# A decoder layer in fp32 on TensorE: the start bytes of the moving operands

## The chip, the cores and the metric

The kernel runs on one core of a Trainium2 chip. The metric is the device time of one execution in microseconds, from the first to the last instruction and what lies around them; the time before is the median of three runs. The profile is one further execution, taken by the hardware profiler.

Five engines work side by side, each in its own order: TensorE (PE; its weight loads are listed apart as PEld), VectorE (DVE), ScalarE (ACT), GpSimd (POOL), and SyncE (SP), which issues the transfers. They wait for each other by semaphores.

## The reference

One layer over 512 positions of width 2048, all in float32:

```python
h = x + W_out [ DilatedAttn(q,k,v) || S5(u) ]   # [q|k|v|u] = RMSNorm(x) W_in, 1024 columns each
h = h + (silu(n @ w_gate) * (n @ w_up)) @ w_down  # n = RMSNorm(h), D_FF = 5632
y = RMSNorm(h)
```

The attention has 8 heads of 128 and mixes three dilations; S5 is a diagonal state space layer over 64 groups, followed by a gelu and a gate `sigmoid(y @ w_glu)`.

## The kernel before, in words

Everything is kept transposed: features on the 128 partitions, the 512 positions along the free axis. A product is a chain of matmuls on a 128 x 128 weight block (the stationary operand) and 512 or 256 columns of an activation (the moving operand).

To reach float32 accuracy each operand is split in two parts: `hi`, a copy rounded to the matmul's fp32r type, which ScalarE makes (L90), and `lo`, the rest, which VectorE makes (L91 through the helper at L50). A product of two such pairs is three matmuls, hi x hi (L109), weight hi x activation lo (L110) and weight lo x activation hi (L111), in `mm3` at L108. Every matmul has its own weight load. Weights stream from HBM in pieces of 512 KB (`raw`, 4 buffers), are split into `whi` and `wlo` (5 buffers each, 512 columns), and are used once.

The split activations live in slots. `laid` at L167 takes a slot of 1088 words (4352 bytes) a partition and returns 1024 of them, hi in the first half and lo in the second, from word `o` on:

```python
    t = pool_.tile([128, SLOT], F32R, tag=tag, name=name, bufs=bufs)
    return t[:, o:o + 1024].rearrange("p (a b) -> p a b", a=2)
```

The slots of all pools start at multiples of 256 bytes (two small pads, of 480 bytes and 992, see to it). So the start byte of a moving operand within 256 bytes is 4 x `o`, for hi and for lo alike. The pools are `A0` and `A1` (8 slots each), `B` (8 slots in `ring2`), and in `mp` the tags `a` and `C` (4 slots each). One slot holds different operands in the course of the program.

The stages, in the order of the program:

- `u`, `q`, `k`, `v`: products with the 16 tiles `x0` to `x15` (in A0 and A1, `o` = 0), 512 columns each; the state space layer runs beside `u` and `k`.
- Attention: scores, softmax, transposes and `po`; its 8 results are split into `attn` (A0, `o` = 8).
- `glu`: 8 output tiles, each 8 chunks of `ysp` (B, `o` = 4), 512 columns; gated results go to `ssm` (A1, `o` = 40).
- `oa`: the attention half of W_out, 16 output tiles x 8 chunks of `attn`, 512 columns.
- `os`: the other half with `ssm`, in two passes over 256 columns each (`os0`, `os1`), 16 output tiles x 8 chunks. Behind each pass the norm of its columns follows.
- `gu`: gate and up of one feed-forward tile `f` of 44. They are computed by a scheme with seven products of 256 columns instead of eight, named by their weights A to G. A and B read the operand set `c1` (A0), C reads `c4` (tag C, `o` = 52), D and F read `c3` (A1), E and G read `c2` (B); the sets c1 to c3 have `o` = 48. A product is 8 chunks of 128 features, 24 matmuls, in two halves of 12: in the steady state the order on PE is A, C, B, D, E, F, G for the first half and again for the second, 168 matmuls a tile. The first five tiles (`first`) have A and B ahead of the others, since c2 to c4 are made only when the second pass's norm is known.
- `dn`: behind the first `gu` tile of each later group of four, in the code; on PE it stands between groups: 16 output tiles x 4 chunks of `m` (tag a, `o` = 0), 512 columns, 192 matmuls. There are ten, `dn0` to `dn9`.
- `dl`: the last down product with the last four `m` (`o` = 48), in two passes of 256 columns, and the final norm.

A scheduler decides the order in which the instructions of one engine stand.

Of the kernel before, what the change touches and what calls it, by code (L numbers as in the profile page):

```python
# [35 lines left out]
def _emit(tc, a, y):  # L36
# [4 lines left out]
    def opened(name, **kw):  # L41
        cm = tc.tile_pool(name=name, **kw)
        open_pools[name] = cm
        return cm.__enter__()
# [4 lines left out]
    def tt(out, in0, in1, op, eng=None):  # L49
        (eng or dve).tensor_tensor(out=out, in0=in0, in1=in1, op=op)  # L50
# [23 lines left out]
    def acc(name):  # L74
        return psum.tile([128, 512], F32, tag="acc", name=name, bufs=5)
# [13 lines left out]
    def split(hi, lo, raw):  # L89
        act.activation(hi, raw, AF.Copy)  # L90
        tt(lo, raw, hi.bitcast(F32), ALU.subtract)  # L91
# [21 lines left out]
    def ftile(ps, chunks, acts, name):  # L113
        n = len(chunks)
        for c, src in enumerate(chunks):
            ws = wchunk(src, f"{name}_{c}")
            for k in range(8):
                hi, lo = ws[k // 4]
                sl = slice(128 * (k % 4), 128 * (k % 4) + 128)
                mm3(ps, hi[:, sl], lo[:, sl], acts[8 * c + k], c == 0 and k == 0, c == n - 1 and k == 7)  # L120
# [43 lines left out]
    ring = opened("ring", bufs=1)  # L164
    SLOT = 1088

    def laid(pool_, tag, name, bufs, o):  # L167

        t = pool_.tile([128, SLOT], F32R, tag=tag, name=name, bufs=bufs)
        return t[:, o:o + 1024].rearrange("p (a b) -> p a b", a=2)  # L170

    def slot(tag, name, shift=0):
        return laid(ring, tag, name, 8, shift)
# [123 lines left out]
    for n in (1, 2, 4):  # L297
# [4 lines left out]
        t_ = pt[:, :, :n]  # L302
# [233 lines left out]
    ring2 = opened("ring2", bufs=1, side="right")  # L536
# [20 lines left out]
    ysp = []  # L557
    for b in range(8):
        yt = wpool.tile([128, 512], F32, tag="sq", name=f"yt{b}", bufs=4)
        nc.sync.dma_start(yt, sy[b].rearrange("p i c -> p (i c)"))  # L560
        t_ = laid(ring2, "B", f"ysp{b}", 8, 4)
        split(t_[:, 0, :], t_[:, 1, :], yt)
        ysp.append(t_)


    attn = []
    def scores(h):
        Pb = [slot("A1", f"P{h}_{i}").bitcast(F32) for i in range(2)]
        Tb = [slot("A1", f"PT{h}_{i}").bitcast(F32) for i in range(2)]
        for i in range(4):  # L570
            n = 128 * (i + 1)
            P = Pb[i // 2][:, i % 2, :]
            sps = aux([128, 512], f"sc{h}_{i}")
            pe.matmul(sps[:, :n], qs[h][:, 128 * i:128 * i + 128], ks[h][:, 0:n], start=True, stop=True)
            st = cpool.tile([128, 4], F32, tag="st", name=f"st{h}_{i}", bufs=4)
            dve.tensor_tensor_reduce(out=P[:, :n], in0=sps[:, :n], in1=mask[:, 512 - n:512], scale=1.0, scalar=-3e38,
                                     op0=ALU.add, op1=ALU.max, accum_out=st[:, 0:1])
            ts(st[:, 1:2], st[:, 0:1], -SCALE)
            act.activation(P[:, :n], P[:, :n], AF.Exp, bias=st[:, 1:2], scale=SCALE, accum_out=st[:, 2:3])
            dve.reciprocal(st[:, 3:4], st[:, 2:3])  # L580
            ts(P[:, :n], P[:, :n], st[:, 3:4])
        return Pb, Tb

    nxt = scores(0)
    for h in range(NH):
        Pb, Tb = nxt
        if h + 1 < NH:
            nxt = scores(h + 1)
        po = acc(f"po{h}")
        for step in "t0 t1 t2 p0 t3 p1 p2 p3".split():  # L590
            j = int(step[1])
            w = 512 - 128 * j
            PT = Tb[j // 2][:, j % 2, :]
            if step[0] == "t":
                tp = acc(f"tp{h}_{j}")
                for i in range(j, 4):
                    pe.transpose(tp[:, 128 * (i - j):128 * (i - j) + 128], Pb[i // 2][:, i % 2, 128 * j:128 * j + 128], ident)
                act.activation(PT[:, :w], tp[:, :w], AF.Copy)
            else:
                pe.matmul(po[:, 128 * j:512], vs[j][:, 128 * h:128 * h + 128], PT[:, :w], start=j == 0, stop=j == 3)  # L600
        o = slot("A0", f"attn{h}", 8)
        act.activation(o[:, 0, :], po, AF.Copy)
        tt(o[:, 1, :], po, o[:, 0, :].bitcast(F32), ALU.subtract)
        attn.append(o)


    ssm = []
    for f in range(8):
        ps = acc(f"glu{f}")
        ftile(ps, [a["w_glu"][f]], ysp, f"glu{f}")  # L610
        g_ = wpool.tile([128, 512], F32, tag="sq", name=f"gate{f}", bufs=4)
        act.activation(g_, ps, AF.Sigmoid, bias=bg[:, f:f + 1])
        yt = wpool.tile([128, 512], F32, tag="sq", name=f"yr{f}", bufs=4)
        nc.sync.dma_start(yt, sy[f].rearrange("p i c -> p (i c)"))
        z = wpool.tile([128, NC_, T], F32, tag="sq", name=f"gz{f}", bufs=4)
        tt(z.rearrange("p c i -> p i c"), yt.rearrange("p (i c) -> p i c", i=T), g_.rearrange("p (i c) -> p i c", i=T), ALU.mult)
        o = slot("A1", f"ssm{f}", 40)
        split(o[:, 0, :], o[:, 1, :], z.rearrange("p c i -> p (c i)"))
        ssm.append(o)
    closed("v")  # L620
# [6 lines left out]
    h = [hall[:, f, :] for f in range(KT)]  # L627
# [10 lines left out]

    def comb(tag, name, pool_=None, bufs=8):

        return laid(pool_ or ring, tag, name, bufs, 52 if tag == "C" else 48).rearrange("p a (h t) -> p a h t", h=2)

    early = {}

# [21 lines left out]
    def first_half(k):  # L666
        n_ = laid(mp, "a", f"n1_{k}", 4, 0).bitcast(F32).rearrange("p a (h t) -> p a h t", h=2) if k % 2 == 0 else n1[-1][1]
        n1.append((n_[:, k % 2], n_))
        tc.keep_in_program_order(norm(n1[k][0][:, 0], k, E[0]))
        norm(n1[k][0][:, 1], k + 8, E[0])  # L670
        t_ = comb("A0", f"c1_{k}")
        split(t_[:, :, 0, :], t_[:, :, 1, :], n1[k][0])
        c1.append(t_)
# [96 lines left out]
    for k in range(8):  # L770
        es = E[1]
        x_, y_, z_ = (wpool.tile([128, 2, 256], F32, tag="sq", name=f"{n}_{k}", bufs=4) for n in ("x2", "t12", "t34"))
        norm(x_[:, 0], k + 8, es)
        norm(z_[:, 0], k, es)
        tt(x_[:, 1], x_[:, 0], z_[:, 0], ALU.subtract, pool)
        t2 = comb("B", f"c2_{k}", ring2)
        split(t2[:, :, 0, :], t2[:, :, 1, :], x_)
        tt(y_[:, 0], z_[:, 0], n1[k][0][:, 0], ALU.subtract, pool)
        tt(y_[:, 1], x_[:, 0], y_[:, 0], ALU.subtract, pool)
        t3 = comb("A1", f"c3_{k}")  # L780
        split(t3[:, :, 0, :], t3[:, :, 1, :], y_)
        tt(z_[:, 1], n1[k][0][:, 1], y_[:, 1], ALU.subtract, pool)
        if k % 2 == 0:
            t4 = comb("C", f"c4_{k}", mp, 4)
            c4.append(t4)
        split(t4[:, k % 2, 0, :], t4[:, k % 2, 1, :], z_[:, 1])
        c2.append(t2)
        c3.append(t3)
# [14 lines left out]
    for p in range(NPH):  # L803
        ms = []
        for q in range(4):
            f = 4 * p + q
# [114 lines left out]
```

## Time and profile before

| | us |
|---|---|
| median of 3 runs | 2116.21 |
| lowest and highest | 2115.62, 2118.56 |
| the profiled execution | 2112.28 |
| its span, first to last instruction | 2110.5 |
| PE busy | 2053.3 (97%) |
| PEld busy | 1858.4 (88%) |
| DVE busy | 1535.6 (73%) |
| ACT busy | 865.6 (41%) |
| mean granted TensorE clock | 0.986 |

A matmul's recorded duration reaches from its start to the modelled end of its last column, and the next one starts before that: in steady state a 256-column matmul is listed with 276 ns and the next starts 113 ns behind its start. What counts for the time is the distance of the starts. An engine listed as busy throughout may still be slower or faster per instruction, so the tables of stretches are read together with the counts and with the mean duration of one.

### The profile page before, as it was taken

What the parts mean: (1) busy time and instruction counts of PE and PEld (TensorE: products, weight loads), DVE (VectorE), ACT (ScalarE), POOL (GpSimd) and SP (SyncE); (2) the same over time, 40 slices, a digit from 0 to 9 for tenths busy, and PEclk for the clock granted to TensorE, in tenths of its full rate; (3) what the DMA queues carried; (4) which work ended last, traced back from release to release, by engine and by line L of the source; (5) the groups of instructions that cost most, each with busy time, mean ns of one, the idle gap of its engine ahead of it and who ended that gap; (6) DMA issues with size and microseconds to landing.
All of it is one profiled execution on the core that took longest, in us unless ns stands there. A gap on an engine that the chain in (4) does not pass through costs nothing.

```text
span 2110.5 us, 35164 instructions
## 1 busy us (share of the span) xinstructions
PE 2053.3 (97%) x13522; PEld 1858.4 (88%) x13522; DVE 1535.6 (73%) x2932; ACT 865.6 (41%) x1523; POOL 198.1 (9%) x172
## 2 busy tenths in 40 slices
PE   7899999999999979999999999999999999999996
PEld 5688888877889979899998989899998989999896
DVE  8835897555436989687786968687686868778686
ACT  5222222346325645344443535344352535444354
POOL 4533102300002360000000000000000000000002
PEclk9999999999999989999999999999999999999998
DMA  6443234623324614323232223323232332323232
GB/s 222 127 121 112 92 102 140 178 81 125 125 91 169 206 65 140 121 100 120 82 129 90 101 101 120 111 90 130 85 124 83 111 110 101 120 88 124 90 121 80
DMA packets 117193, 244.24 MB, mean 116 GB/s; under 512 B 39040, under 2 KB 57312, under 8 KB 117024
## 3 DMA queue, kind: packets, MB, share of 16 engines
q1 hardware_dynamic: 107808, 239.88, 33.8%
q10 hardware_dynamic: 9216, 2.10, 0.5%
q8 instruction: 106, 1.74, 0.3%
q14 instruction: 63, 0.52, 0.1%
HBM read 229.77 MB, written 9.03 MB: 113 GB/s over the span
## 4 chain that ended last, share of the span: by engine, by line
PE 87%; DVE 7%; issue 2%; DMA 1%; ACT 1%; SPq 0%; POOL 0%; DVEq 0%; ACTq 0%; POOLq 0%
PE gu L109 12%; PE gu L111 12%; PE gu L110 12%; PE dn L110 7%; PE dn L109 7%; PE dn L111 7%; PE lps L437 1%; PE q L111 1%; PE q L110 1%; PE oa L111 1%; PE oa L109 1%; PE oa L110 1%; PE q L109 1%; PE v L550 1%; PE v L552 1%
## 5 line engine op out<-in xcount | busy, mean ns | idle before, releaser
L110 PE MATMUL dn<-m,whi_dn 128*128 128x512 f32 x640 | 249.0, 389 | 0.0
L109 PE MATMUL dn<-m,whi_dn 128*128 128x512 f32 x640 | 248.8, 389 | 0.0
L111 PE MATMUL dn<-m,wlo_dn 128*128 128x512 f32 x640 | 248.8, 389 | 0.0
L50 DVE TENSOR_TENSOR h<-h,dn 128x512 f32<-128x512 f32 x160 | 109.9, 687 | 172.5 <-PE dn L111 171.3
L90 ACT ACTIVATE whi_dn<-raw_dn 128x512 fp32r<-128x512 f32 x160 | 100.9, 632 | 240.5 <-PE dn L110 208.2
L50 DVE TENSOR_TENSOR raw_r<-raw_r,raw_r 128x512 f32<-128x512 f32 x264 | 182.5, 691 | 2.2
L111 PEld LDWEIGHTS dn<-m,wlo_dn 128*128 128x128 f32 x640 | 120.2, 188 | 24.9
L109 PEld LDWEIGHTS dn<-m,whi_dn 128*128 128x128 f32 x640 | 120.2, 188 | 24.6
L110 PEld LDWEIGHTS dn<-m,whi_dn 128*128 128x128 f32 x640 | 120.2, 188 | 24.5
L50 POOL TENSOR_TENSOR h<-h,ssf 128x256 f32<-128x256 f32 x12 | 10.7, 920 | 1300.1 <-ACT ssf L160 1300.1
L50 DVE TENSOR_TENSOR wlo_dn<-raw_dn,whi_dn 128x512 fp32r<-128x512 f32 x160 | 109.8, 687 | 17.6 <-ACT whi_dn L90 16.5
L109 PE MATMUL gu<-c,whi_C 128*128 128x256 f32 x352 | 99.8, 284 | 1.9 <-ACT c L90 1.6
L111 PE MATMUL gu<-c,wlo_E 128*128 128x256 f32 x352 | 98.8, 281 | 2.8 <-DVE wlo_E L50 2.8
L109 PE MATMUL gu<-c,whi_D 128*128 128x256 f32 x352 | 98.3, 279 | 2.7 <-ACT whi_D L90 2.7
L109 PE MATMUL gu<-c,whi_E 128*128 128x256 f32 x352 | 98.5, 280 | 2.4 <-ACT whi_G L90 1.7
L111 PE MATMUL gu<-c,wlo_D 128*128 128x256 f32 x352 | 98.5, 280 | 2.0 <-DVE wlo_D L50 2.0
L111 PE MATMUL gu<-c,wlo_C 128*128 128x256 f32 x352 | 99.5, 283 | 0.5 <-DVE wlo_C L50 0.5
L110 PE MATMUL gu<-c,whi_C 128*128 128x256 f32 x352 | 99.6, 283 | 0.1
L110 PE MATMUL gu<-c,whi_E 128*128 128x256 f32 x352 | 98.3, 279 | 0.0
L110 PE MATMUL gu<-c,whi_D 128*128 128x256 f32 x352 | 98.0, 278 | 0.0
L109 PE MATMUL gu<-c,whi_F 128*128 128x256 f32 x352 | 97.7, 277 | 0.0
L109 PE MATMUL gu<-c,whi_G 128*128 128x256 f32 x352 | 97.5, 277 | 0.2 <-ACT whi_G L90 0.2
(323 smaller groups left out, 6673.1 us busy)
## 6 DMA issues: line engine op xcount, KB each, us to landing
raw_r<-w_gu SPq DMA_DIRECT2D x176, 512.0 KB, 3.6
raw_dn<-w_down SPq DMA_DIRECT2D x80, 512.0 KB, 4.1
raw_os<-w_out SPq DMA_DIRECT2D x32, 512.0 KB, 3.4
raw_q<-w_q SPq DMA_DIRECT2D x16, 512.0 KB, 3.5
raw_k<-w_k SPq DMA_DIRECT2D x16, 512.0 KB, 3.4
raw_v<-w_v SPq DMA_DIRECT2D x16, 512.0 KB, 3.7
raw_oa<-w_out SPq DMA_DIRECT2D x16, 512.0 KB, 3.5
raw_u<-w_u SPq DMA_DIRECT2D x15, 512.0 KB, 4.7
```

The lines of the kernel that those rows point to most:

```text
L50: (eng or dve).tensor_tensor(out=out, in0=in0, in1=in1, op=op)
L90: act.activation(hi, raw, AF.Copy)
L109: pe.matmul(ps, wh, x[:, 0, :], start=first, stop=False)
L110: pe.matmul(ps, wh, x[:, 1, :], start=False, stop=False)
L111: pe.matmul(ps, wl, x[:, 0, :], start=False, stop=last)
L437: pe.matmul(lps[:, g, :], tm_[:, :, :, g].rearrange("p i q -> p (i q)"), U[:, 8 * b + g, :], start=True, stop=True)
L550: pe.matmul(pss[m], xs[kt][:, 0, ms], wh, start=kt == 0, stop=False)
L552: pe.matmul(pss[m], xs[kt][:, 1, ms], wh, start=False, stop=kt == 15)
```

## The change

Four start offsets go; no other line changes. The order of instructions on PE, DVE, ACT, POOL and SP is the same row for row, and the slots are at the same addresses.

```diff
-        t_ = laid(ring2, "B", f"ysp{b}", 8, 4)
+        t_ = laid(ring2, "B", f"ysp{b}", 8, 0)
...
-        o = slot("A0", f"attn{h}", 8)
+        o = slot("A0", f"attn{h}")
...
-        o = slot("A1", f"ssm{f}", 40)
+        o = slot("A1", f"ssm{f}", 48)
...
-        return laid(pool_ or ring, tag, name, bufs, 52 if tag == "C" else 48).rearrange("p a (h t) -> p a h t", h=2)
+        return laid(pool_ or ring, tag, name, bufs, 48).rearrange("p a (h t) -> p a h t", h=2)
```

In bytes: `ysp` goes from 16 to 0, `attn` from 32 to 0, `ssm` from 160 to 192, and `c4`, the operand of product C, from 208 to 192. Behind it every operand read in 256 columns starts at byte 192 of its slot (or 1024 and 2048 bytes further), and every one read in 512 columns at byte 0.

## Rows read from the trace of the kernel before

**Rows 1.** The page: span, busy time of the engines.

```profile
span 2110.5 us, 35164 instructions
PE 2053.3 (97%) x13522; PEld 1858.4 (88%) x13522; DVE 1535.6 (73%) x2932; ACT 865.6 (41%) x1523; POOL 198.1 (9%) x172
```

**Rows 2.** Five stretches: busy time of each engine, granted clock, DMA share.

```profile
core 0: us, PE busy (x) PEld busy (x) DVE busy (x) ACT busy (x) POOL busy (x), PEclk, DMA share, GB/s
640.00:685.00 45.00, 45.00 (x377) 45.00 (x377) 28.67 (x48) 25.90 (x48) 11.33 (x14) 1.00 0.52 177
698.00:734.00 36.00, 34.32 (x278) 33.13 (x278) 35.78 (x63) 22.43 (x45) 14.11 (x13) 1.00 0.54 182
760.00:800.00 40.00, 28.37 (x166) 25.58 (x166) 38.26 (x57) 17.19 (x32) 22.27 (x20) 0.79 0.23 79
800.00:856.00 56.00, 54.23 (x455) 53.16 (x456) 54.18 (x100) 29.73 (x51) 0.00 (x0) 1.00 0.38 134
901.10:978.00 76.90, 76.90 (x673) 76.90 (x672) 64.93 (x114) 39.68 (x66) 0.00 (x0) 1.00 0.33 115
```

**Rows 3.** Matmuls by shape: count, busy us, mean ns; last two: 745 to 757, 2055.5 to 2070.3.

```profile
L109 PE MATMUL dn<-m,whi_dn 128*128 128x512 f32 x640 | 248.8, 389 | 0.0
L110 PE MATMUL glu<-ysp,whi_glu 128*128 128x512 f32 x64 | 25.2, 394 | 0.0
L110 PE MATMUL oa<-attn,whi_oa 128*128 128x512 f32 x128 | 50.6, 395 | 0.0
L110 PE MATMUL os<-ssm,whi_os 128*128 128x256 f32 x256 | 72.2, 282 | 0.0
L109 PE MATMUL gu<-c,whi_C 128*128 128x256 f32 x352 | 99.8, 284 | 1.9 <-ACT c L90 1.6 <-DVE gt L50 0.2
L109 PE MATMUL gu<-c,whi_F 128*128 128x256 f32 x352 | 97.7, 277 | 0.0
...
L110 PE MATMUL gu<-c,whi_A 128*128 128x256 f32 x12 | 3.4, 281 | 0.0
...
L111 PE MATMUL dl<-m,wlo_dl 128*128 128x256 f32 x45 | 12.3, 276 | 0.0
```

**Rows 4.** Timeline of PE behind `dn3`: start us, duration us, instruction; first of five blocks.

```profile
1141.97 0.28 PE L109 MATMUL gu<-c,whi_A 128*128 128x256 f32 x1
...
1143.39 0.28 PE L109 MATMUL gu<-c,whi_C 128*128 128x256 f32 x1
...
1144.81 0.28 PE L109 MATMUL gu<-c,whi_B 128*128 128x256 f32 x1
...
1146.19 0.28 PE L109 MATMUL gu<-c,whi_D 128*128 128x256 f32 x1
...
1151.63 0.28 PE L109 MATMUL gu<-c,whi_A 128*128 128x256 f32 x1
```

**Rows 5.** Timeline of PE in the fourth tile's E and F, and in `dl`.

```profile
839.64 0.28 PE L110 MATMUL gu<-c,whi_E 128*128 128x256 f32 x1
...
841.41 0.28 PE L110 MATMUL gu<-c,whi_G 128*128 128x256 f32 x1
...
2083.80 0.39 PE L109 MATMUL dl<-m,whi_dl 128*128 128x256 f32 x1 [1.17 <-DVE h L50]
2084.03 0.28 PE L110 MATMUL dl<-m,whi_dl 128*128 128x256 f32 x1
...
2085.91 0.28 PE L111 MATMUL dl<-m,wlo_dl 128*128 128x256 f32 x1
```

**Rows 6.** Timeline of PE: ends of the first and of the last group.

```profile
901.10 0.28 PE L109 MATMUL gu<-c,whi_A 128*128 128x256 f32 x1
...
978.00 0.39 PE L109 MATMUL dn<-m,whi_dn 128*128 128x512 f32 x1
...
1985.05 0.28 PE L109 MATMUL gu<-c,whi_A 128*128 128x256 f32 x1
...
2044.44 0.28 PE L109 MATMUL dl<-m,whi_dl 128*128 128x256 f32 x1
```

## The prediction

> **What bounds the kernel now.** I read the page's engine shares first, then a table of stretches, then the matmuls grouped by shape, then the timeline of single matmuls. The shares: TensorE is busy for 97% of the span, weight loads for 88%, VectorE for 73% [rows 1]. The stretches show where that means a bound [rows 2]. From 901.1 to 978 us, the first of ten such groups of four gate/up tiles, PE is busy for 76.90 of 76.90 us and VectorE for 64.93: no wait, every nanosecond on a matmul counts. The first `os` pass (640 to 685) is the same. The second `os` pass (698 to 734) and the making of the operands after the norm (760 to 800) are VectorE's: 35.78 of 36 us and 38.26 of 40, PE idle beside it. From 800 to 856 both are near full (54.23 and 54.18 of 56).
>
> So the question is the distance from one matmul to the next, and whether the start address of the moving operand sets it. The groups by shape [rows 3] have durations: a 512-column matmul takes 389 ns in `dn` (byte 0), 394 in `glu` (byte 16), 395 in `oa` (byte 32). A 256-column one takes 277 ns in `gu` F (byte 192), 284 in `gu` C (byte 208) and 282 in `os` (byte 160). That alone reads as: the four odd offsets cost 5 to 7 ns a matmul, and the change takes this away.
>
> The next rows say that this reading is not enough. At byte 192 there are two paces, not one. In rows 3 the `A` products between 745 and 757 us, at byte 192, take 281 ns; the `dl` products between 2055.5 and 2070.3, at byte 192, take 276; same clock, no wait in either. The timeline of the first tile behind `dn3` [rows 4] shows what chooses. A starts at 1141.97, C at 1143.39, B at 1144.81, D at 1146.19, and the second A at 1151.63. Twelve A's (byte 192) take 1.42 us, 118 ns each; twelve C's (byte 208) 1.42 us, 118; twelve B's (byte 192 again) 1.38 us, 115 on average, the first four near 119 and the rest at 113; and the 48 of D, E, F, G 5.44 us, 113.3 each. So A behind a 512-column product runs at the slow pace although its offset is the "good" one, and the pace falls to the fast one only behind C. All ten groups of tiles that follow a `dn` begin so; the tiles that follow a `gu` tile begin fast.
>
> **Does the slow pace end by itself?** Everything hangs on this. The runs at byte 192 in which it appears with no C in them: 745 to 757 [rows 3], E and F from 839.64 to 841.41 (15 matmuls in 1.77 us), and the closing product, which restarts at 2083.80 after a wait of 1.17 us on VectorE and then holds 1.88 us for 16 matmuls from 2084.03 to 2085.91 [rows 5], and so on to 2091. In all some 300 matmuls at the slow pace, ended by a wait, by C or by the end; none falls to the fast pace alone, and none of the stretches at the fast pace rises alone. Together with A's twelve the three measured pieces are 5.07 us for 43 matmuls, 117.9 ns. It looks like two stable paces of the same stream, kept by whatever the matmul's read and the weight load beside it do to each other, and the pace is inherited. C at byte 208 is slow itself, but whatever pace enters it, the fast one leaves. For 512 columns at byte 0 I see no second pace: `dn` ends at 389 ns whatever came before.
>
> **The change, part by part.** No instruction is added, removed or reordered on any engine; slots and their bases stay. Only start bytes inside the slot move. The writers (ScalarE and VectorE, eight of a kind per stage) get no price: they lie beside a full PE in every stage but the VectorE-bound ones, and there only `c4`'s eight halves move.
>
> 1. `ysp` 16 to 0: 3 x 64 = 192 matmuls, 394 to 389 ns: -1.0 us, on the path.
> 2. `attn` 32 to 0: 3 x 128 = 384 matmuls, 395 to 389: -2.3 us, on the path.
> 3. `ssm` 160 to 192, 768 matmuls. The first pass is entered from a 512-column product at byte 0, as A is entered from `dn`, so I expect the slow pace. Before, 45.00 us hold 377 matmuls, of which two had started earlier [rows 2]: 120.0 ns each, against 117.9: 384 x 2.1 = -0.8 us (bounds 0, and 384 x 6 = -2.3 at the fast pace). The second pass is VectorE's; of its 0.8 us I take -0.2, for the tiles ahead of 698 us.
> 4. `c4` 208 to 192 in the first five tiles. Between 800 and 856 there are 455 matmuls; were all to go from 113.3 to 117.9, that is +2.1 us, with 1.77 us of PE idle to hide it, and C's own gain against it. Bounds -0.5 and +2.1; I take +1.0, nearer to the full price since VectorE is as late as PE there.
> 5. `c4` in the 39 tiles from 901.10 on. This is the large term. Before: a group of four takes 978.00 - 901.10 = 76.90 us; nine such (the others agree to 0.02) are 692.1; the last three tiles run from 1985.05 to 2044.44, 59.39 us, with 15 `dl` matmuls among their 504 [rows 6]. Together 751.5 us for 6567 matmuls, 114.4 each. After: the group still enters through A at the slow pace, since `dn` and A are untouched. C at 192 is then twelve more matmuls of the same kind, and nothing is left in the group that gives back the fast pace. 6567 x 117.9 = 774.2 us: **+22.7 us**. PE has no wait there to hide it in, and VectorE, with 12 us to spare in each group, gets only more slack.
> 6. The closing product: some 40 matmuls up to its first wait, +0.2; behind it every restart may take either pace (bounds -0.7 and +0.7).
>
> Sum: -1.0 - 2.3 - 0.8 - 0.2 + 1.0 + 22.7 + 0.2 = +19.6 us. The profiled execution took 2112.28 us (span 2110.5), so 2131.9 for its like; it lies 3.9 us under the median of the three timed runs, 2116.21, and on that scale the forecast is 2135.8, **2136 us: slower by 0.9%**.
>
> **A rule against it.** Neighbouring products of one tile, equal in columns and clock, stand at 277 and 284 ns with only the start byte between them [rows 3]. The Trainium skill, "TensorE: Matmul & The Clock Gate", section "Step-by-step: what each phase is for", holds that the moving operand and the weight load have independent read ports, so that loading the next weights takes no read bandwidth from the running matmul; the Trainium skill, "SBUF — State Buffer", section "Specifications (TRN2)", gives lines of 16 bytes. By these all the offsets here, multiples of 16, are alike and the change does nothing, 2116 us; the trace disagrees by the 7 ns just named. It is rival N below.
>
> **Rivals.**
> - B, the plain reading: byte 192 is fast and the slow pace does not outlive A. Then every 256-column matmul goes to 113.3: term 5 is 6567 x 113.3 = 744.1, -7.4; terms 1 and 2 as above, -3.3; `os` -2.3 and -0.7; the first tiles -0.5; in all -14.2, 2102 us. For it: most of the trace at byte 192 is fast. Against: those rows all stand behind a C or a wait.
> - P, the slow pace lasts for part of a group. With a share s of the 6567 slow, term 5 is 744.1 + 30.2 s - 751.5; with the other terms (-3.1) the sign turns at s = 0.35. Above it, 2116 to 2131; below, 2105 to 2116. The eight slots of `c4` begin at other bases than `c1`'s, which could still move the pace.
> - N, nothing moves: the paces belong to the products and their place in the program, not to the offset, so all stay as they are: 2116. For it: each odd offset occurs in one product only. Against it: `attn` lies in the slots in which `x` lay, and `dn` at byte 0 is 6 ns shorter than `oa` [rows 3].
> - W, on top of the forecast the half-clock stretch grows: between 760 and 800 the granted clock is 0.79 [rows 2], so part ran at 1.2 GHz while PE waited for VectorE. If it lasts 10 us longer at half pace, +5: 2141.
>
> **How the numbers follow.** Forecast 0.76, B 0.08, P 0.08, N 0.04, W 0.04. The forecast's own range is 2130 to 2140 (terms 3, 4, 6 at their ends, and some 2 us of scatter among the timed runs). Downward I take in N and the upper part of P, upward W: 2114 to 2142, which leaves out B and the low part of P. About 0.2% (4 us) is what a measurement of this kernel can tell from no change. Slower by more: the forecast, W and most of P, 0.83; faster: B and the low end of P, 0.11; same 0.06.
>
> **What would show it.** In the changed kernel's profile: `gu` D, E, F, G at 281 ns instead of 277 and the group of four from A to the next `dn` at 79.2 us instead of 76.90 (term 5); `oa` and `glu` at 389 (terms 1, 2); `os` in the first pass at 281 (term 3). If D to G stand at 276 behind C, term 5 is wrong and with it the sign; if C alone stays at 281 or more, the offset is not what made it slow.

## The result, and the profile after

The changed kernel takes 2136.26 us (median of 4 runs, 2135.12 to 2136.65) beside 2115.91 (4 runs, 2113.49 to 2118.56) of the kernel before on the same chip: a ratio of 1.0095 with the interval 1.0078 to 1.0112, slower by 20 us. The profiled execution of it took 2136.65 us.

The page after, to be held against [rows 1]:

```profile
span 2134.9 us, 35164 instructions
PE 2078.5 (97%) x13522; PEld 1884.5 (88%) x13522; DVE 1540.4 (72%) x2932; ACT 865.4 (41%) x1523; POOL 198.6 (9%) x172
```

The counts are the same. PE and its loads are busier by 25 and 26 us, about as much as the span grew (24), VectorE by 5: the same matmuls take longer.

The stretches after, with the columns of [rows 2]; the borders are moved to the same places of the program, and the first row is the start of the program:

```profile
core 0: us, PE busy (x) PEld busy (x) DVE busy (x) ACT busy (x) POOL busy (x), PEclk, DMA share, GB/s
0.00:150.00 150.00, 129.19 (x649) 103.91 (x650) 104.89 (x194) 52.98 (x95) 69.64 (x57) 0.90 0.53 160
...
647.00:685.00 38.00, 38.00 (x325) 38.00 (x325) 23.87 (x40) 21.68 (x41) 10.79 (x13) 1.00 0.53 182
699.00:735.00 36.00, 33.50 (x278) 32.22 (x278) 35.99 (x64) 23.24 (x48) 15.45 (x13) 1.00 0.54 190
762.00:802.00 40.00, 28.32 (x164) 25.42 (x162) 38.10 (x56) 17.10 (x31) 22.18 (x20) 0.79 0.23 79
802.00:858.00 56.00, 54.41 (x444) 53.16 (x445) 52.71 (x98) 28.50 (x49) 0.00 (x0) 0.97 0.39 132
904.43:983.57 79.14, 79.14 (x673) 79.14 (x672) 65.46 (x114) 39.62 (x66) 0.00 (x0) 1.00 0.33 112
```

The last row answers to 901.10 to 978.00 of [rows 2]: the same 672 matmuls, PE without a gap in both, and 79.14 us in place of 76.90. VectorE is busy for the same 65 us.

The matmuls by shape after (count, busy us, mean ns), as in [rows 3]:

```profile
L109 PE MATMUL dn<-m,whi_dn 128*128 128x512 f32 x640 | 248.8, 389 | 0.0
L110 PE MATMUL glu<-ysp,whi_glu 128*128 128x512 f32 x64 | 24.9, 389 | 0.0
L110 PE MATMUL oa<-attn,whi_oa 128*128 128x512 f32 x128 | 49.8, 389 | 0.0
L110 PE MATMUL os<-ssm,whi_os 128*128 128x256 f32 x256 | 71.7, 280 | 0.0
L109 PE MATMUL gu<-c,whi_C 128*128 128x256 f32 x352 | 99.5, 283 | 1.6 <-ACT c L90 1.6
L109 PE MATMUL gu<-c,whi_F 128*128 128x256 f32 x352 | 100.2, 285 | 0.0
```

`glu` and `oa` went to 389 ns, as `dn`. `C` stayed where it was, 284 to 283, although its offset was corrected; `F`, whose operand was not touched, went from 277 to 285. (The means of `gu` hold a few matmuls that start after a wait; inside a group one takes 281.)

The timeline of PE after: the two ends of the first group, and then the tile that [rows 4] show before the change, the first behind the third `dn` (`dn2` when counted from `dn0`; [rows 4] and the prediction call it `dn3`); first matmul of a block each time:

```profile
904.42 0.28 PE L109 MATMUL gu<-c,whi_A 128*128 128x256 f32 x1
...
983.57 0.39 PE L109 MATMUL dn<-m,whi_dn 128*128 128x512 f32 x1
...
1149.76 0.28 PE L109 MATMUL gu<-c,whi_A 128*128 128x256 f32 x1
...
1151.17 0.28 PE L109 MATMUL gu<-c,whi_C 128*128 128x256 f32 x1
...
1152.59 0.28 PE L109 MATMUL gu<-c,whi_B 128*128 128x256 f32 x1
...
1154.00 0.28 PE L109 MATMUL gu<-c,whi_D 128*128 128x256 f32 x1
...
1155.41 0.28 PE L109 MATMUL gu<-c,whi_E 128*128 128x256 f32 x1
...
1159.65 0.28 PE L109 MATMUL gu<-c,whi_A 128*128 128x256 f32 x1
```

Twelve matmuls of A, of C, of B and of D take 1.41 or 1.42 us each, 118 ns a matmul; half a tile takes 9.89 us where it took 9.66. The 113 ns of D to G are gone from the whole group, and from the three tiles behind it: every group lasts 79.15 us from its first A to the next `dn`.

The difference by stages, each measured from the start of its first matmul to that of the next stage's (us, before to after): `u`, here with the 6 us ahead of its first matmul, 154.17 to 160.15; `q` 117.40 both; `k` to attention 232.51 and 232.52; `glu` 45.44 to 44.54; `oa` 89.60 to 87.04; `os0` 46.08 to 45.23; `os1` 49.40 to 49.12; first five tiles and `dn0` 166.50 to 168.43; nine groups of four, 76.90 to 79.15 each; each `dn` between them 43.53 to 43.52; last three tiles 59.39 to 61.13; the rest of the closing product and the end 66.06 to 65.32. `u`'s 6 us are not the change's: nothing in it is touched, and the same stage took between 154.2 and 162.1 us over the thirteen profiles. Where it is long, the granted clock at its start is lower: the first 150 us have 0.93 where `u` took 154.2 and 0.89 where it took 161.9 and 162.1. It is 0.90 in the stretch above, and in the kernel before:

```profile
0.00:150.00 150.00, 128.06 (x668) 104.52 (x669) 106.09 (x195) 53.45 (x96) 69.76 (x57) 0.93 0.54 161
```

From `k`'s first matmul to the end, which leaves that out, the difference is 1838.94 to 1857.32, **+18.4 us**. This number, called the tail below, is the better measure for kernels with a single run. It still holds the scatter of the stages in which VectorE is late and of the closing product, some us: e3 and e11 below differ by 0.97 us in the stage that was edited, and by 5.2 in their tails.

### The profile page after: what moved, and what is told of

Read it like the earlier page. It is cut to its first block, busy times and chain, and to the rows that moved or that the text cites. A ratio compares the mean times of both kernels' runs of the same rounds, so it can differ in the third digit from the quotient of the medians.

```text
span 2134.9 us, 35164 instructions
## 1 busy us (share of the span) xinstructions
PE 2078.5 (97%) x13522; PEld 1884.5 (88%) x13522; DVE 1540.4 (72%) x2932; ACT 865.4 (41%) x1523; POOL 198.6 (9%) x172
## 4 chain that ended last, share of the span: by engine, by line
PE 88%; DVE 6%; issue 2%; DMA 1%; ACT 1%; POOL 0%; SPq 0%; DVEq 0%; ACTq 0%; POOLq 0%
PE gu L109 13%; PE gu L111 13%; PE gu L110 12%; PE dn L111 7%; PE dn L110 7%; PE dn L109 7%; PE lps L437 1%; PE q L111 1%; PE q L110 1%; PE q L109 1%; PE v L550 1%; PE v L552 1%; PE k L109 1%; PE k L110 1%; PE k L111 1%
## 5 line engine op out<-in xcount | busy, mean ns | idle before, releaser
L50 DVE TENSOR_TENSOR wlo_dn<-raw_dn,whi_dn 128x512 fp32r<-128x512 f32 x160 | 109.8, 687 | 20.3 <-ACT whi_dn L90 19.1
L109 PE MATMUL gu<-c,whi_C 128*128 128x256 f32 x352 | 99.5, 283 | 1.6 <-ACT c L90 1.6
L111 PE MATMUL gu<-c,wlo_F 128*128 128x256 f32 x352 | 100.0, 284 | 0.2 <-DVE wlo_F L50 0.2
L109 PE MATMUL gu<-c,whi_F 128*128 128x256 f32 x352 | 100.2, 285 | 0.0
L110 PE MATMUL gu<-c,whi_F 128*128 128x256 f32 x352 | 100.0, 284 | 0.0
```

The source lines that it names most:

```text
L109: pe.matmul(ps, wh, x[:, 0, :], start=first, stop=False)
L110: pe.matmul(ps, wh, x[:, 1, :], start=False, stop=False)
L111: pe.matmul(ps, wl, x[:, 0, :], start=False, stop=last)
```

## The experiments

All have the same instructions in the same order on each engine as the two kernels; only start bytes differ (in e7 and e10 the size of the weights' tiles too). The slow pace is 117.8 ns from start to start of 256-column matmuls, the fast one 113.3. Each ratio is to runs of the kernel before on the same chip; a kernel without a ratio has one run, and its time holds the scatter of `u`. `dn`, `oa`, `os0` and the group of four are in us, for the first of its kind (of `dn`, the first that nothing interrupts, `dn1`).

| kernel | time, us | ratio to before (interval) | tail, us | group of four | `dn` | `oa` | `os0` |
|---|---|---|---|---|---|---|---|
| before | 2115.91 | | 1838.9 | 76.90 | 43.53 | 89.60 | 46.08 |
| after | 2136.26 | 1.0095 (1.0078 to 1.0112) | 1857.3 | 79.15 | 43.52 | 87.04 | 45.23 |
| e1: `c4` alone | 2137.83 | 1.0107 (1.0090 to 1.0124) | 1860.4 | 79.15 | 43.52 | 89.60 | 46.08 |
| e2: all but `c4` | 2114.98 | 0.9992 (0.9980 to 1.0005) | 1835.8 | 76.90 | 43.53 | 87.04 | 45.23 |
| e3: one slot at 208 | 2107.51 | 0.9963 (0.9952 to 0.9974) | 1834.2 | 76.50 | 43.53 | 87.04 | 45.23 |
| e4: last chunk of `dn` at 208 | 2117.27 | | 1838.8 | 76.16 | 44.56 | 87.04 | 45.23 |
| e5: `m`, `attn` at 192 | 2115.66 | | 1840.5 | 76.16 | 44.80 | 89.60 | 43.53 |
| e6: everything at 0 | 2149.86 | | 1874.9 | 80.63 | 43.55 | 87.04 | 46.07 |
| e7: weights at 16 | 2160.72 | | 1880.2 | 79.74 | 44.80 | 87.04 | 45.62 |
| e8: `m`, `attn` at 64 | 2141.80 | | 1860.7 | 79.15 | 43.96 | 87.91 | 45.22 |
| e9: `m`, `attn` at 128 | 2124.74 | | 1843.4 | 76.16 | 44.80 | 89.59 | 43.52 |
| e10: weights at 16 ahead of the group | 2133.05 | 1.0084 (1.0068 to 1.0099) | 1859.3 | 79.15 | 43.52 | 87.04 | 45.23 |
| e11: e3 and one slot of `ssm` | 2108.95 | 0.9962 (0.9949 to 0.9976) | 1829.0 | 76.50 | 43.53 | 87.04 | 44.26 |

### The change in two halves

e1 is the kernel before with one edit:

```diff
-        return laid(pool_ or ring, tag, name, bufs, 52 if tag == "C" else 48).rearrange("p a (h t) -> p a h t", h=2)
+        return laid(pool_ or ring, tag, name, bufs, 48).rearrange("p a (h t) -> p a h t", h=2)
```

Expected:

> Only c4 moves from byte 208 to 192; ysp, attn and ssm stay at 16, 32 and 160. Theory (the slow pace is inherited from dn and only C at 208 ended it): the loss is c4's alone, +1.0 in the first tiles, +22.7 in the 39 tiles, +0.2 at the end, so 2116 + 24 = 2140 us; a group of four from A to the next dn takes 79.2 us, products D to G 281 ns. Rival (the loss comes from the pace in which glu, oa and os leave the engine, that is from the other three offsets): c4 alone gains its own 1056 x 5 ns, about 2110 us, the group 76.2.

e2 is the changed kernel with that line put back, so that only `ysp`, `attn` and `ssm` have moved. Expected:

> ysp, attn and ssm move, c4 stays at byte 208. Theory: terms 1 to 3 alone, -1.0 -2.3 -0.8 -0.2 = -4.3, so 2112 us; glu and oa at 389 ns, os in its first pass at 281, the group of four unchanged at 76.90 us. Rival (the loss comes from these three): 2136 us, the group at 79.

The ends of the first group in e1's timeline of PE:

```profile
907.01 0.28 PE L109 MATMUL gu<-c,whi_A 128*128 128x256 f32 x1
...
986.15 0.39 PE L109 MATMUL dn<-m,whi_dn 128*128 128x512 f32 x1
```

and in e2's:

```profile
902.73 0.28 PE L109 MATMUL gu<-c,whi_A 128*128 128x256 f32 x1
...
979.63 0.39 PE L109 MATMUL dn<-m,whi_dn 128*128 128x512 f32 x1
```

79.14 and 76.90 us: `c4`'s offset alone makes the loss, and with `c4` at 208 the group is as it was. In the tails the halves add up: +21.4 for e1 and -3.2 for e2, +18.2 together, where the whole change has +18.4. e2's gain was expected at 4.3 us; `glu`, `oa` and `os0` did shorten (0.92, 2.56 and 0.85 us), but the stages behind them, `os1` and the first five tiles, where VectorE is late, are 0.67 and 0.75 longer in its profile. The total is not separable from no change: 0.9992, the interval holds 1.

### How little of byte 208 the fast pace needs

e3 is the changed kernel with one of the four slots of `c4` at byte 208:

```diff
-        return laid(pool_ or ring, tag, name, bufs, 48).rearrange("p a (h t) -> p a h t", h=2)
+        return laid(pool_ or ring, tag, name, bufs, 52 if name == "c4_2" else 48).rearrange("p a (h t) -> p a h t", h=2)
```

Expected:

> As the changed kernel, but one of the four c4 slots (chunks 2 and 3, six matmuls of the first half of C) lies at byte 208, the others at 192. Theory (any matmuls at 208 end the slow pace): only the first 28 matmuls of a group are slow, then every tile pays some 10 x 5 ns; the group takes about 76.45 us, -0.45 x 9.75 = -4.4, and with -4.3 from the other three about 2107 us, faster than both kernels. Rival (a whole C of 24 at 208 is needed, or its slots at both parities): the group stays at 79.2, 2136 us.

e3's timeline of PE; the row at 905.62 is the first of the six matmuls of this tile that read the slot at 208:

```profile
903.50 0.28 PE L109 MATMUL gu<-c,whi_A 128*128 128x256 f32 x1
...
904.91 0.28 PE L109 MATMUL gu<-c,whi_C 128*128 128x256 f32 x1
...
905.62 0.28 PE L109 MATMUL gu<-c,whi_C 128*128 128x256 f32 x1
...
906.33 0.29 PE L109 MATMUL gu<-c,whi_B 128*128 128x256 f32 x1
...
907.04 0.28 PE L109 MATMUL gu<-c,whi_B 128*128 128x256 f32 x1
...
980.00 0.39 PE L109 MATMUL dn<-m,whi_dn 128*128 128x512 f32 x1
```

Twelve of A and six of C at 118 ns (2.12 us), six at 208 in 0.71 us (118), six more behind them in 0.71, and then 113.3. The other three tiles of the group enter fast, and each has its own six matmuls at 208 and the six behind them at about 119: 76.50 us in all. So 24 of the 672 matmuls are at 208, and the first six of them end the slow pace. The kernel is 8.9 us faster than before in the medians (2116.40 in the 19 runs of before on that chip): nine groups shorter by 0.40 would be 3.6 of it, `glu`, `oa` and `os0` 4.3, and the last three tiles 0.3. Its profile has all of these, but is longer by 3.5 in `os1`, the first five tiles and the closing product, so that the tail is only 4.7 shorter; how the 8.9 us divide is not shown.

### What `dn` hands over

e4 is the changed kernel with the last of `dn`'s four chunks at 208, so that each output tile of `dn` ends with three matmuls at 208:

```diff
-        o = laid(mp, "a", f"m{f}", 4, 48 * (f >= 4 * (NPH - 1)))
+        o = laid(mp, "a", f"m{f}", 4, 48 if f >= 4 * (NPH - 1) else 52 if f % 4 == 3 else 0)
```

Expected:

> As the changed kernel, but the last of the four m that a dn product reads lies at byte 208 instead of 0, so that each dn ends with three matmuls of 512 columns at 208. It costs 48 x 5 ns in each of ten dn, +2.4 us. Theory (the pace of a group is inherited from how the last dn matmul ends): the group may now start at the fast pace and then keeps it, 76.15 us, 2116 - 4.3 - 7.4 - 0.5 + 2.4 = 2106 us. Rival (the step from 512 to 256 columns alone sets the slow pace): the group stays at 79.2, 2139 us.

e4's timeline of PE, the end of a `dn` and the group behind it:

```profile
903.42 0.40 PE L109 MATMUL dn<-m,whi_dn 128*128 128x512 f32 x1
...
904.13 0.28 PE L109 MATMUL gu<-c,whi_A 128*128 128x256 f32 x1
...
904.47 0.28 PE L109 MATMUL gu<-c,whi_A 128*128 128x256 f32 x1
...
980.29 0.39 PE L109 MATMUL dn<-m,whi_dn 128*128 128x512 f32 x1
```

The first three A's take 0.34 us, 113 each, and the group 76.16 us, 672 x 113.3: the fast pace throughout, with all of A to G at 192 as in the changed kernel. So A was slow for what stood ahead of it. The price was underrated: `dn` costs 1.03 us more, not 0.24, since the nine matmuls behind the three also go slower (224 to 238 ns apart where `dn` at byte 0 has 226.7). That leaves the total where the kernel before is.

e5, e8 and e9 put all of `m` and of `attn` at one other multiple of 64, 192, 64 and 128:

```diff
-        o = slot("A0", f"attn{h}")
+        o = slot("A0", f"attn{h}", 48)
...
-        o = laid(mp, "a", f"m{f}", 4, 48 * (f >= 4 * (NPH - 1)))
+        o = laid(mp, "a", f"m{f}", 4, 48)
```

with 16 and 32 in place of the 48 in e8 and e9 (the last four `m` kept at 48). Expected:

> As the changed kernel, but m of every dn and attn of oa lie at byte 192 too, so no product from oa on steps from byte 0 to byte 192 any more (glu, u, q, k, v stay at 0). Theory (the pace of a group comes from how dn hands over, not from the step in columns): if 512 columns at 192 run at 227 ns as they do at 0, a group of four starts and stays at the fast pace, 76.15 us instead of 79.15, os in its first pass at 276 instead of 281, in all 2136 - 9.75 x 3.0 - 1.7 = 2105 us. Rival (the step from 512 to 256 columns sets the slow pace wherever both start): 79.15 us, 2136 us. Third case: 512 columns at 192 have a slow pace of their own; then dn lies above 43.5 us.

> As the changed kernel, but attn and the m of every dn lie at byte 64, the operands of 256 columns stay at 192. Theory (the start bytes of dn's and oa's last matmuls set the pace of what follows): the group of four is either 76.16 us (fast, as behind byte 192) or 79.15 (slow, as behind byte 0), with nothing between, and os in its first pass 43.5 or 45.2 in the same way. If 512 columns at 64 run at 227 ns (dn 43.5, oa 87.0) and hand over the fast pace, all stages are at their best: 2136 - 29.2 - 1.7 = 2105 us. Rival (the pace behind dn is set by something else than its start byte, and byte 192 is special by being the same as what follows): 79.15 and 45.2, 2136 us.

> The same with attn and m at byte 128. Theory: again 76.16 or 79.15 and 43.5 or 45.2, and the pace of the 512 columns at 128 tells whether multiples of 64 bytes share the 227 ns of byte 0 (192 did not: 231 to 236). 2105 us if they do and hand over the fast pace. Rival: 79.15 and 45.2 whatever the byte, so long as it is not 192: 2136 us.

`dn` in e5's matmuls by shape:

```profile
L109 PE MATMUL dn<-m,whi_dn 128*128 128x512 f32 x640 | 252.9, 395 | 0.0
```

and in e9's:

```profile
L109 PE MATMUL dn<-m,whi_dn 128*128 128x512 f32 x640 | 252.6, 395 | 0.0
```

512 columns at 128 or 192 take 395 ns instead of 389 (44.80 us for 192, 233 apart), and the group that follows has the fast pace from its first matmul, 76.16. At 64 they cost 43.96, and the group is slow, 79.15. The first and last rows of e9's first group:

```profile
908.66 0.28 PE L109 MATMUL gu<-c,whi_A 128*128 128x256 f32 x1
...
984.82 0.40 PE L109 MATMUL dn<-m,whi_dn 128*128 128x512 f32 x1
```

The rival of e9, that only 192 would hand the fast pace over, is wrong: 128 does so as well. In `oa` and `os0` the same pairs return: `oa` at 0 or 64, `os0` 45.2; `oa` at 128 or 192, `os0` 43.5. Wherever all of A to G are at 192 and the weights at 0 (after, e1, e4, e5, e8 to e10), a group has one of two lengths, 76.16 or 79.15, and what ran ahead of it picks which. Against the changed kernel, e5's `dn` loses ten times 1.28 us and its `oa` 2.56, while its groups gain nine times 2.99 and `os0` 1.70; that brings it back to the kernel before (tail +1.6) and no further.

### Is it the byte, or the stream?

e6 moves all 256-column operands to byte 0 as well:

```diff
-        o = slot("A1", f"ssm{f}", 48)
+        o = slot("A1", f"ssm{f}")
...
-        return laid(pool_ or ring, tag, name, bufs, 48).rearrange("p a (h t) -> p a h t", h=2)
+        return laid(pool_ or ring, tag, name, bufs, 0).rearrange("p a (h t) -> p a h t", h=2)
...
-        o = laid(mp, "a", f"m{f}", 4, 48 * (f >= 4 * (NPH - 1)))
+        o = laid(mp, "a", f"m{f}", 4, 0)
```

Expected:

> As the changed kernel, but the operands read in 256 columns lie at byte 0 as well (ssm, c1 to c4, the last four m), so all moving operands start at byte 0. Theory (two paces belong to the stream of weight load and matmul, not to byte 192): 113.3 and 117.9 ns show again, and whichever the entry gives is kept: 2136 us if dn hands over the slow one, 2105 if the fast one. Rival (256 columns at 0 have one pace only): every product, behind a wait too, has the same mean duration, 276 or more.

The ends of the first group in e6's timeline:

```profile
901.96 0.28 PE L109 MATMUL gu<-c,whi_A 128*128 128x256 f32 x1
...
982.59 0.40 PE L109 MATMUL dn<-m,whi_dn 128*128 128x512 f32 x1
```

80.63 us for 672 matmuls, 120.0 ns each. At byte 0 the 256-column stream has one pace, slower than both of byte 192, and it does not depend on the entry: of the 384 matmuls of `dl`, many of them behind a wait, 349 have the next one 120 ns behind them and none 113. So two paces are not a property of any 256-column stream; the start byte decides whether there are two.

e7 leaves the moving operands of `mm3` as in the changed kernel and starts the split weights 16 bytes into their tiles, all but the early ones of the first tiles and those of `dl`. (In `v` the weights are the moving operand; it runs there at the 232 ns that `glu` had at byte 16 before the change.)

```diff
-        hi, lo = (wpool.tile([128, 512], F32R, tag=t, name=f"{t}_{name}", bufs=HB) for t in ("whi", "wlo"))
+        hi, lo = (wpool.tile([128, 576], F32R, tag=t, name=f"{t}_{name}", bufs=HB)[:, 4:516] for t in ("whi", "wlo"))
```

(and likewise the two that are made by hand for the first product). Expected:

> As the changed kernel, but the split weights of wsplit lie 16 bytes into slots of 2304 bytes (the early and the last weights stay), so that the distance between the start of the weight load and that of the moving operand is what it was for an operand 16 bytes lower, while the operand's own start is unchanged. Theory A (what counts is the distance between the two reads): the matmuls change their duration, 512 columns at 0 from 389 to 394 or so and 256 columns at 192 to 282 or so as c4 at 208 had, without the fast pace of 276. Theory B (the moving operand's own start byte counts): as the changed kernel, 389 and 281, 2136 us.

By shape in e7, `dn` and `oa`:

```profile
L110 PE MATMUL dn<-m,whi_dn 128*128 128x512 f32 x640 | 254.4, 397 | 0.0
...
L110 PE MATMUL oa<-attn,whi_oa 128*128 128x512 f32 x128 | 49.8, 389 | 0.0
```

Neither theory had this: A has the longer `dn`, but not the `glu` and `oa` that stay. The weight's start byte does take part: 512 columns at byte 0, which had one pace before, now have two, 227 ns in `glu` and `oa` (44.59 and 87.04 us) and 233 in `dn` (44.80 us). The larger tiles are not the reason, for e10 below has them too, with `dn` at 43.52. The group is at 79.74, 118.7 a matmul.

Both paces stand within one product of e7, `q`, at a granted clock of 1.00 each time:

```profile
159.53 0.39 PE L109 MATMUL q<-x,whi_q 128*128 128x512 f32 x1
...
164.97 0.39 PE L109 MATMUL q<-x,whi_q 128*128 128x512 f32 x1
...
179.43 0.40 PE L109 MATMUL q<-x,whi_q 128*128 128x512 f32 x1
...
182.23 0.40 PE L109 MATMUL q<-x,whi_q 128*128 128x512 f32 x1
```

The 24 matmuls of the first pair are 226.7 ns apart; the 12 of the second, behind several pauses of PE and a stretch at the granted clock 0.50, 233.3. Operands and weights have the same start bytes in both, so the bytes alone do not set the pace here.

e10 tries to use that: the weights of the last 24 matmuls of each `dn` and of `oa` at 16, all others at 0, to have the group entered by a slower product:

```diff
-        hi, lo = (wpool.tile([128, 512], F32R, tag=t, name=f"{t}_{name}", bufs=HB) for t in ("whi", "wlo"))
+        o = 4 if name.startswith("oa15_") or name.startswith("dn") and "_7_" in name else 0; hi, lo = (wpool.tile([128, 576], F32R, tag=t, name=f"{t}_{name}", bufs=HB)[:, o:o + 512] for t in ("whi", "wlo"))
```

Expected:

> As the changed kernel with all operands at 0 and 192, but the split weights of each dn's last chunk (its last two output tiles, 24 matmuls) and of oa's last output tile lie 16 bytes into their slots; slots of 2304 bytes for all weights. Theory (the pace of the group comes from how the last matmuls before it end, and the weight load's start byte takes part in that): those 24 matmuls run near 233 ns, +0.15 us per dn, and what follows takes one of the two paces: fast, 76.16 us a group and 43.5 in os, 2136 - 29.2 - 1.7 + 1.6 = 2107 us, or slow again, 79.15 and 45.2, 2138. Rival (the operand's start byte alone counts): 79.15 and 45.2, no change in dn, 2136.

e10's first group:

```profile
904.06 0.28 PE L109 MATMUL gu<-c,whi_A 128*128 128x256 f32 x1
...
983.21 0.39 PE L109 MATMUL dn<-m,whi_dn 128*128 128x512 f32 x1
```

No effect: `dn` 43.52, the group 79.15, the ratio within the interval of the changed kernel's. A 512-column stream that runs at 227 stays there when the weights move to 16, so the slower `dn` of e7 does not come from the weights' byte alone: with `q` in e7, this says that 512 columns too can keep a pace that they enter with.

### The version that beats both

e11 adds to e3 the same trick for `os`: the first slot of `ssm` at 208.

```diff
-        o = slot("A1", f"ssm{f}", 48)
+        o = slot("A1", f"ssm{f}", 48 if f else 52)
```

Expected:

> As the run with one c4 slot at byte 208, and the first of the eight ssm also at 208 instead of 192. Theory (a few matmuls at 208 end the slow pace in any 256-column stream): in the first pass of os each output tile pays some 8 x 5 ns for the three matmuls and those behind, in place of 24 x 4.6, so os0 takes about 44.1 us instead of 45.23 and the whole is 1 us under the 2107.5 of one slot: 2106.5. Rival (three matmuls are too few): os0 stays at 45.2 or goes up, 2107.5 to 2108.

`os0` in e11's timeline, from its first matmul to the first of `os1`:

```profile
638.75 0.28 PE L109 MATMUL os<-ssm,whi_os 128*128 128x256 f32 x1
...
683.01 0.28 PE L109 MATMUL os<-ssm,whi_os 128*128 128x256 f32 x1
```

44.26 us instead of 45.23, as expected, but in the total not to be told from e3 (0.9962 and 0.9963). Both are faster than the kernel before by 0.4%, and by the two ratios than the changed one by 1.3%.

## Why the prediction was right

The forecast was 2136 us, and the medians gave 2136.26. By its terms:

- Terms 1 to 3 (`ysp`, `attn`, `ssm`: -1.0, -2.3, -0.8, -0.2): measured -0.9, -2.6, -0.85 and -0.28 in their stages, `glu` and `oa` at 389 ns and `os0` at the slow pace, as said. e2 adds that part of it is lost again behind them, in stages that VectorE bounds; the prediction took the gain in full.
- Term 4 (+1.0 in the first five tiles): +1.9 in the two profiles. Up to `dn0`'s first matmul the five tiles took 121.9 to 123.7 us in the six kernels with all of their operands at 192 (after, e1, e5, e8, e9, e10), and 121.8 and 122.6 in the two with all of `c4` at 208 (before, e2), so its size stays within the scatter.
- Term 5 (+22.7) is the step on which everything hung: that the slow pace has no end of its own, and C at 208 was what ended it. It held: 79.15 us against 79.2, in all nine groups, D to G at 281 ns, and e1 and e3 show C's offset alone to be the cause. The size was a little high: 9 x 2.25 = 20.3 against 21.0, and 1.7 for the last three tiles against 1.8, together 22.0 us.
- Term 6 (+0.2): -0.7 from the end of the last three tiles on, at its lower bound. This stretch took 65.2 to 67.6 us over the thirteen profiles, so that is scatter.

The sum, +19.6, stands against +18.4 in the tail and +20.4 in the medians. The mechanism and the size of term 5 are no luck; that the median lies within 0.3 us of 2136 is. Terms 4 and 6 missed by 0.9 us each in opposite directions, and runs of one kernel differ by several us.

Of the rivals, B (byte 192 is fast, 2102 us) and P (the slow pace lasts part of a group) fell with D to G at 281: the share s is 1. N fell with `glu`, `oa` and `F`, which all moved with start bytes, theirs or a neighbour's. W did not come: the stretch before the first tiles has the granted clock 0.79 in both. (P speaks of eight slots of `c4`; there are four.)

Two rules stand behind N. By the Trainium skill, "TensorE: Matmul & The Clock Gate", section "Step-by-step: what each phase is for", the weight load takes nothing from the running matmul's reads. The trace does not bear this out as a rule on speed: in e7 the weights of `dn` moved by 16 bytes and its operands stayed, and its 192 matmuls went from 43.52 to 44.80 us. By the Trainium skill, "SBUF — State Buffer", section "Specifications (TRN2)", lines are 16 bytes long, and by that alone all these offsets would be alike. The trace disagrees: six matmuls a tile at 208 instead of 192 moved the group by 2.65 us (e3).

Two statements were too wide. "For 512 columns at byte 0 I see no second pace" is true of these two kernels; e7 has a second one, with other weight addresses. And "A behind a 512-column product runs at the slow pace" holds for 512 columns at 0 and 64, not at 128 and 192 (e5, e9), nor where `dn` at 0 ends with three matmuls at 208 (e4).

What stays open is the reason. The runs show that the pace of a stream depends on the start byte of its moving operand, on that of its weights and on the pace of what ran ahead; they do not show what in the chip keeps the two paces apart, nor why a restart after a wait takes one or the other.

## What to carry to other kernels

Where TensorE is never idle, read the distance of matmul starts block by block in order of time, not the mean by product: the mean put the blame on the one operand that set the others right. A start byte is then to be tested together with its neighbours' and with the block that runs ahead, and a short block at another offset may be worth more than it costs (six matmuls at 208 in each tile here). An offset that is best for one product can be paid for in the next one: `dn` is fastest at 0, and hands the slow pace on.

## What was unexpected

- The start bytes do not sort by alignment. 256 columns behind a 512-column product: 120.0 ns at byte 0 (e6) and at 160 (`os0` before, 46.08 us for 384), 113.3 or 117.8 at 192. 512 columns, with the weights at 0: 226.7 at 0, 229 at 64, 233 at 128 and 192, and also at 32 (`oa` before, 89.60 us for 384).
- A stream at 192 keeps the pace that it was handed over 672 matmuls and 79 us, and six matmuls at 208 end the slow one (e3).
- The runs of one kernel lie up to 9 us apart (before, 19 runs: 2111.77 to 2121.02). In the profiles the first stage shows most of that: `u` took 154.2 us in one and 162.1 in another, though nothing in it was changed but in e7 and e10, and of the two shown above the longer one has the lower granted clock in it.
